# A hybrid decoder layer on one core: the merge, output projection and gate with ScalarE and VectorE in program order, and small operands prepared at other places

## The chip, the core and the metric

The kernel runs on one core of a Trainium2 chip. The core has a matrix engine (TensorE, "PE" in the profile), whose weight loads are listed apart as PEld, a vector engine (VectorE, "DVE"), a scalar engine for pointwise functions and copies (ScalarE, "ACT"), GpSimd ("POOL") and SyncE ("SP"). In this kernel GpSimd issues most weight transfers and SyncE the other transfers. The metric is the device time of one execution in microseconds (us). Before the change three runs took 463.31 to 463.59 us, with a median of 463.48 us.

## What is computed

One layer (DEPTH is 1) of a decoder on 512 tokens of width 1024. Cut to its steps:

```python
xn = rmsnorm(h, norm_gain)
aq, ak, av, ag, bq, bf, bi, bg, gate_a, gate_b = split(xn @ w_in)
ya = moba_attention(rmsnorm(aq), rmsnorm(ak), av, rel_bias)     # 8 heads x 64
ya = (ya * silu(ag)) @ w_up_a
yb = hgrn2_chunkwise(silu(bq), kb, bi, log_f)                   # 4 heads x 128
yb = (rmsnorm(yb) * silu(bg)) @ w_up_b
merged = sigmoid(gate_a) * ya + sigmoid(gate_b) * yb
h = h + merged @ w_out
ple = (p @ w_ple) * sigmoid(h @ w_ple_gate)
h = h + ple
```

All tensors are float32. Each float32 product is made of three products of rounded halves, so every operand of a matmul is first split into a high and a low part.

## The kernel before

**Splits.** `split(hi, lo, src)` (L192 to L194) is one ScalarE copy that rounds `src` to the high part (L193) and one VectorE subtraction that leaves the low part (L194). The names in the profile follow it: a raw weight `wf` becomes `wh` and `wl`; the merged rows become `mh` and `ml`; the new `h` (`hf`) becomes `hh` and `hl`; the transposed embedding `pf` becomes `ph` and `pl`; the gate's small weights `w_ple`, kept in `pb`, become `pwh` and `pwl`; the two branches' outputs become `yah`, `yal`, `ybh`, `ybl`. `mm3` (L247 to L254) multiplies: for each slice k of 128 rows it issues three matmuls of 128x512 (high by high, low by high, high by low weight), and it then ticks a planner's clock by 3 x 0.227.

**Weights.** All 80 weight tiles have a fixed sequence. `weight(ap)` returns tile i, but first loads raw tiles up to i + 2 and splits them. There are two raw buffers and three buffers each of `wh` and `wl`, so the load of tile i + 2 waits for the split of tile i, and the copy of tile i + 2 waits for the last product with tile i - 1. In the stretch at issue tiles 48 to 55 belong to the up-projections of the recurrent branch (`ub0` to `ub7`), 56 to 63 to those of attention (`ua0` to `ua7`; 128x512 each), 64 to 71 to the output projection (`h0` to `h7`; 128x1024) and 72 to 79 to the gate (`g0` to `g7`; 128x1024).

**The last stages.** `up(0, n, ya, ...)` makes `ua` number n in 12 matmuls. VectorE multiplies it by the sigmoid of gate a (L914) and adds the other branch (L915), and the result `sga` is split into `mh` and `ml` number n. Then each `h` number n needs all eight `mh` and `ml` (24 matmuls); VectorE adds the residual `xres` (L927), and the sum is split into `hh` and `hl`. Last, each `g` number n needs all eight `hh` and `hl` (24 matmuls), and beside it `pe` number n (6 matmuls) multiplies p with the small weights; ScalarE takes the sigmoid of `g`, VectorE multiplies and adds, and SyncE stores.

**The recurrence.** For each of four heads the planner runs a generator beside the projections. `hgrn_intra` builds score blocks in the PSUM banks `lpb` and `lpa`. `hgrn_out` then transposes a key block (`hktp`), copies it out by ScalarE (`hkt`, L598), multiplies it (`hds`, L603), forms the states on VectorE (L607, L610), and makes the output `hop` (L616, L618). ScalarE squares `hop` (L622); a normalisation follows that goes between VectorE and ScalarE (`npart`, `nquad`, `nms`, `nt`, `ny`, `nwide`, lines 272 to 293), and VectorE reads `hop` for the last time in L624. The banks of the tag "g" are two, so `lpa` of the next head takes the bank that L624 gives back. A `yield` in these generators is a number of microseconds of the planner's clock until the generator goes on; it sets between which matmuls its own matmuls stand.

**Attention.** `scores` (L709) makes logits `s`; the softmax runs over VectorE (L726, L729), ScalarE (L728, L730) and a VectorE transpose (L733); SyncE moves the result by 16 transfers per step within `pb` (L744); the product with the values is `o` (L757).

**What sets the order.** PE's instructions stand in the order in which the program traces them, with the planner's clock deciding where the generators' pieces go. ScalarE, VectorE, GpSimd and SyncE are ordered by a scheduler that simulates a timeline and takes what is ready by priority; `tc.high_priority(offset=AHEAD)` raises the priority of the merge. On the chip each engine works through its list in that order.

Of the kernel before, what the change touches and what calls it, by code (L numbers as in the profile page):

```python
# [20 lines left out]
KD = D // 128  # L21
# [36 lines left out]
def hybrid_layer_kernel(  # L58
# [530 lines left out]
    def hgrn_out(h, vb):  # L589
# [6 lines left out]
        cost(0.33)  # L596
        kts = unit("KT", f"hkt{h}")
        A.activation(kts[:, :nk], kt[:, :nk], AF.Copy)  # L598
        yield 4.0
        hv = slice(h * 128, h * 128 + 128)  # L600
        dsp = bank("g", f"hds{h}")
        for c in range(3):
# [288 lines left out]
    for kind, i in ORDER:  # L891
        if kind == "bf":
            head(i)
        elif kind == "bg":
            sbgs.append(silu_block(12 + i, f"bg{i}"))
        elif kind == "ag":
            sags.append(silu_block(8 + i, f"ag{i}"))
        elif kind == "ub":
            drain(f"yb{GH - 1}")
            ps = up(1, i, yb, f"ub{i}")  # L900
            V.tensor_tensor(sg["gb", i], ps, sg["gb", i], op=OP.mult)
        else:
            ps = proj_tr({"ga": 16, "gb": 24}[kind] + i, f"{kind}{i}")
            sg[kind, i] = unit("A" if kind == "ga" and i < 4 else "H", f"s{kind}{i}")
            sigmoid(sg[kind, i], ps)
    mh, ml = [], []
    for n in range(KD):
        ga, gb = sg["ga", n], sg["gb", n]
        drain(f"ya{HPAIRS - 1}")
        ps = up(0, n, ya, f"ua{n}")  # L910
        h_ = unit("YB", f"mh{n}", R)
        l_ = unit("A", f"ml{n}", R)
        with tc.high_priority(offset=AHEAD):
            V.tensor_tensor(ga, ps, ga, op=OP.mult)  # L914
            V.tensor_tensor(ga, ga, gb, op=OP.add)  # L915
            split(h_, l_, ga)
        mh.append(h_)
        ml.append(l_)
    hh, hl, hf = [], [], []
    for n in range(KD):  # L920
        ws = weight(w_o[n])
# [9 lines left out]
        hh.append(h_)  # L931
        hl.append(l_)
        hf.append(t)
    ph, pl = [], []
    for k in range(2):
        t = unit("A", f"pf{k}")
        for i in range(2 - k):
            w = 256 * (1 + k)
            nc.sync.dma_start(t[:, w * i:w * i + w], pT[:, k, w * i:w * i + w])
        h_ = unit("A", f"ph{k}", R)  # L940
        l_ = unit("A", f"pl{k}", R)
        split(h_, l_, t)
        ph.append(h_)
        pl.append(l_)
    for n in range(KD):
        if n % 2 == 0:
            pw = pb[:, n // 2].rearrange("p (a b c) -> p a b c", a=2, b=2)
            nc.sync.dma_start(pw, w_p[n // 2])
            pwh = unit("SG", f"pwh{n}", R, (128, 2, 2, 128))
            pwl = unit("T", f"pwl{n}", R, (128, 2, 2, 128))  # L950
            split(pwh, pwl, pw)
        ws = weight(w_g[n])
        pe = bank("a", f"pe{n}")
        parts = 1 if n < KD - 1 else 2
        w = 512 // parts
        for i in range(parts):
            s_ = slice(i * w, i * w + w)

            def ple():
                mm3(pe[:, s_], pwh[:, n % 2], pwl[:, n % 2], [a[:, s_] for a in ph], [a[:, s_] for a in pl], 2)  # L960

            last = i == 1
            if not last:
                ple()
            ps = bank("mm", f"g{n}_{i}")
            mm3(ps[:, :w], ws[0], ws[1], [a[:, s_] for a in hh], [a[:, s_] for a in hl], KD)
            if last:
                ple()
            t = unit("Q", f"sg{n}_{i}")
            A.activation(t[:, :w], ps[:, :w], AF.Sigmoid)  # L970
            V.tensor_tensor(t[:, :w], t[:, :w], pe[:, s_], op=OP.mult)
            V.tensor_tensor(t[:, :w], t[:, :w], hf[n][:, s_], op=OP.add)
            nc.sync.dma_start(out[n][:, s_], t[:, :w])
# [66 lines left out]
```

## Time and profile before

| what | value |
|---|---|
| runs | 463.31, 463.48, 463.59 us |
| the profiled execution, its own time | 463.43 us |
| its span in the profile | 461.7 us |
| TensorE busy | 454.5 us, 98% of the span |
| PE weight loads | 375.9 us, 81% |
| VectorE busy | 297.7 us, 64% |
| ScalarE busy | 276.3 us, 60% |
| `ua` (first to last start) | 335.5 to 357.1 us |
| `h` | 357.3 to 402.9 us |
| `pe` and `g` | 402.9 to 457.7 us |

The span runs from the first to the last recorded instruction; 1.73 us of the execution lie outside it. In the timeline views a row gives the start, the duration, the engine, the line, the operation, the output and inputs, their shapes and a count; in brackets stands how long the engine was idle before and what ended that. Matmuls of 128x512 overlap: each is listed with 0.39 us, while one starts every 0.227 us.

### The profile page before, as it was taken

The page shows a single profiled execution, that of the slowest core. Times are in us where ns is not written, and L with a number is a line of the kernel's source. Part 1 is how long each engine was busy: PE and PEld are TensorE (multiplying, and loading weights), DVE is VectorE, ACT ScalarE, POOL GpSimd, SP SyncE. Part 2 cuts the span into 40 slices and gives each one's busy share as a digit, 9 for nine tenths or more (in the row PEclk, how much of TensorE's full clock was granted, in tenths as well). Part 3 has the DMA queues.
Part 4 walks back from the last instruction along what each step waited for, and adds up shares of the span by engine and source line. Part 5 has one row for each costly group of instructions (what it writes and reads, how often), then busy time and mean ns, then how long its engine had stood idle before and what let it go on. Part 6 is the DMA issues. An engine that isn't in the chain of part 4 may idle for free.

```text
span 461.7 us, 8102 instructions
## 1 busy us (share of the span) xinstructions
PE 454.5 (98%) x3106; PEld 375.9 (81%) x3106; DVE 297.7 (64%) x604; ACT 276.3 (60%) x532; POOL 38.5 (8%) x77
## 2 busy tenths in 40 slices
PE   9999999999999999999999999999999899999996
PEld 8787888888888888788878888878888688888886
DVE  5668593876888594969686945454469644544222
ACT  5758574747689795979788777774334423322201
POOL 1000100000000101000101000001121100000000
PEclk9999999999999999999999999999999999999999
DMA  7822242220412525162415351335334554222211
GB/s 241 296 91 100 92 136 92 91 92 22 146 65 91 161 99 177 23 182 96 134 56 156 93 179 52 115 119 148 121 91 147 185 165 144 91 103 83 89 45 45
DMA packets 23590, 53.72 MB, mean 116 GB/s; under 512 B 4352, under 2 KB 9728, under 8 KB 23552
## 3 DMA queue, kind: packets, MB, share of 16 engines
q0 software_dynamic: 9056, 32.51, 21.3%
q1 hardware_dynamic: 14352, 20.70, 14.4%
q8 instruction: 24, 0.39, 0.4%
q14 instruction: 14, 0.11, 0.1%
q10 hardware_dynamic: 144, 0.01, 0.0%
HBM read 45.86 MB, written 2.10 MB: 104 GB/s over the span
## 4 chain that ended last, share of the span: by engine, by line
PE 86%; DMA 5%; ACT 5%; issue 2%; DVE 1%; SPq 1%; POOL 0%; POOLq 0%; DVEq 0%; ACTq 0%
PE ga L252 10%; PE g L252 9%; PE gb L252 9%; PE h L252 8%; PE bq L252 5%; PE ak L382 5%; PE ub L252 5%; PE aq L382 5%; PE bf L252 5%; PE bg L252 4%; PE av L382 4%; PE bi L382 4%; PE ag L252 3%; PE pe L252 2%; DMA wf<-in_w_tok_dram 2%
## 5 line engine op out<-in xcount | busy, mean ns | idle before, releaser
L193 ACT ACTIVATE wh<-wf 128x1024 fp32r<-128x1024 f32 (+1 forms) x78 | 75.6, 970 | 102.1 <-PE g L252 20.9
L194 DVE TENSOR_TENSOR wl<-wf,wh 128x1024 fp32r<-128x1024 f32 (+1 forms) x78 | 86.6, 1112 | 64.1 <-ACT wh L193 63.6
L226 POOL DMA_DIRECT2D wf<-in_w_tr_dram x30 | 15.9, 530 | 175.0 <-DVE wl L194 156.6
L252 PE MATMUL g<-hh,wh 128*128 128x512 f32 (+1 forms) x72 | 26.3, 365 | 0.0
L252 PE MATMUL g<-hl,wh 128*128 128x512 f32 (+1 forms) x72 | 26.3, 365 | 0.0
L252 PE MATMUL g<-hh,wl 128*128 128x512 f32 (+1 forms) x72 | 26.3, 365 | 0.0
L252 PE MATMUL h<-ml,wh 128*128 128x512 f32 x64 | 25.0, 391 | 0.8 <-DVE ml L194 0.8
L252 PE MATMUL ga<-xh,wh 128*128 128x512 f32 x64 | 25.7, 401 | 0.0
L252 PE MATMUL h<-mh,wh 128*128 128x512 f32 x64 | 25.0, 391 | 0.5 <-ACT mh L193 0.5
L252 PE MATMUL gb<-xh,wh 128*128 128x512 f32 x64 | 25.0, 391 | 0.0
L252 PE MATMUL ga<-xh,wl 128*128 128x512 f32 x64 | 25.0, 390 | 0.0
L252 PE MATMUL ga<-xl,wh 128*128 128x512 f32 x64 | 25.0, 390 | 0.0
L252 PE MATMUL gb<-xh,wl 128*128 128x512 f32 x64 | 24.9, 389 | 0.0
L252 PE MATMUL gb<-xl,wh 128*128 128x512 f32 x64 | 24.9, 389 | 0.0
L252 PE MATMUL h<-mh,wl 128*128 128x512 f32 x64 | 24.9, 389 | 0.0
L728 ACT ACTIVATE pb<-pb,ps 128x128 f32<-128x128 f32 (+3 forms) x32 | 17.6, 552 | 9.7 <-DVE ps L726 9.6
L726 DVE CUSTOM_DVE_ANT_0 pb<-s,bias 128x128 f32<-128x128 f32 (+3 forms) x28 | 12.8, 496 | 10.2 <-PE s L709 10.0
L927 DVE TENSOR_TENSOR hf<-h,xres 128x512 f32<-128x512 f32 x8 | 5.5, 692 | 18.0 <-PE h L252 18.0
L497 ACT ACTIVATE hx<-hx 128x512 f32<-128x512 f32 x24 | 14.8, 622 | 1.9 <-DVE hx L496 1.8
L730 ACT ACTIVATE pb<-pb,ps 128x128 f32<-128x128 f32 (+3 forms) x32 | 15.8, 550 | 0.0
L252 PEld LDWEIGHTS g<-hl,wh 128*128 128x128 f32 x72 | 13.6, 189 | 2.2
L252 PEld LDWEIGHTS g<-hh,wl 128*128 128x128 f32 x72 | 13.6, 189 | 2.2
(343 smaller groups left out, 1250.3 us busy)
## 6 DMA issues: line engine op xcount, KB each, us to landing
wf<-in_w_tr_dram POOLq DMA_DIRECT2D x30, 512.0 KB, 4.0
wf<-in_w_tok_dram POOLq DMA_DIRECT2D x8, 512.0 KB, 3.6
wf<-in_w_up_dram POOLq DMA_DIRECT2D x16, 256.0 KB, 3.0
wf<-in_w_o_dram POOLq DMA_DIRECT2D x8, 512.0 KB, 4.1
wf<-in_w_g_dram POOLq DMA_DIRECT2D x8, 512.0 KB, 3.5
wf<-in_w_tok_dram SPq DMA_DIRECT2D x6, 512.0 KB, 3.8
pb<-pb SPq DMA_DIRECT2D x64, 48.0 KB, 2.6
bias<-in_ed_dram SPq DMA_DIRECT2D x8, 256.0 KB, 5.0
```

The source lines that it names most:

```text
L193: A.activation(hi, src, AF.Copy)
L194: V.tensor_tensor(lo, src, hi.bitcast(F32), op=OP.subtract)
L226: (G if len(wraw) >= FAR else nc.sync).dma_start(raw, ap)
L252: PE.matmul(ps, a[:, k, :], b[k], start=(n == 0), stop=(n == tot - 1))
L382: PE.matmul(banks[t], a[:, s_], b[:, kk, :], start=(k == 0 and i == 0), stop=(k == KD - 1 and i == 2))
L497: A.activation(x, x, AF.Exp)
L726: in_order(V.tensor_tensor_reduce(p_, s_[:, so:so + nk], T[j][:, nk - 1::-1], -1.0, 3e38, OP.add, OP.min, st[:, 0:1]))
L728: A.activation(p_, p_, AF.Exp, bias=st[:, 0:1], scale=-1.0, accum_out=st[:, 1:2])
L730: A.activation(p_, p_, AF.Copy, scale=st[:, 2:3])
L927: V.tensor_tensor(t, ps, xres, op=OP.add)
```

## The change

It has three parts.

1. In `hgrn_out` the wait between the copy of `hkt` and the product `hds` is 5.0 instead of 4.0 on the planner's clock.
2. From attention's up-projections on, ScalarE and VectorE too stand in the order of the program (`manual_schedule`); the raised priority of the merge is gone with that.
3. The transfers and splits of p (`positions`) are traced behind `h3` and `h4` instead of behind `h7`; the split of the first small weight (`ple_weight`) is traced behind `h5`, and the others one pair of gate tiles ahead, behind the products of `g0`, `g2` and `g4`.

```diff
--- before.py
+++ after.py
@@ -596,7 +596,7 @@
         cost(0.33)
         kts = unit("KT", f"hkt{h}")
         A.activation(kts[:, :nk], kt[:, :nk], AF.Copy)
-        yield 4.0
+        yield 5.0
         hv = slice(h * 128, h * 128 + 128)
         dsp = bank("g", f"hds{h}")
         for c in range(3):
@@ -903,6 +903,8 @@
             ps = proj_tr({"ga": 16, "gb": 24}[kind] + i, f"{kind}{i}")
             sg[kind, i] = unit("A" if kind == "ga" and i < 4 else "H", f"s{kind}{i}")
             sigmoid(sg[kind, i], ps)
+    ctx.enter_context(tc.manual_schedule(engines={mybir.EngineType.Activation, mybir.EngineType.DVE}))
+
     mh, ml = [], []
     for n in range(KD):
         ga, gb = sg["ga", n], sg["gb", n]
@@ -910,12 +912,34 @@
         ps = up(0, n, ya, f"ua{n}")
         h_ = unit("YB", f"mh{n}", R)
         l_ = unit("A", f"ml{n}", R)
-        with tc.high_priority(offset=AHEAD):
-            V.tensor_tensor(ga, ps, ga, op=OP.mult)
-            V.tensor_tensor(ga, ga, gb, op=OP.add)
-            split(h_, l_, ga)
+        V.tensor_tensor(ga, ps, ga, op=OP.mult)
+        V.tensor_tensor(ga, ga, gb, op=OP.add)
+        split(h_, l_, ga)
         mh.append(h_)
         ml.append(l_)
+    ph, pl = [], []
+
+    def positions(k):
+        t = unit("A", f"pf{k}")
+        for i in range(2 - k):
+            w = 256 * (1 + k)
+            nc.sync.dma_start(t[:, w * i:w * i + w], pT[:, k, w * i:w * i + w])
+        h_ = unit("A", f"ph{k}", R)
+        l_ = unit("A", f"pl{k}", R)
+        split(h_, l_, t)
+        ph.append(h_)
+        pl.append(l_)
+
+    pws = {}
+
+    def ple_weight(n):
+        pw = pb[:, n].rearrange("p (a b c) -> p a b c", a=2, b=2)
+        nc.sync.dma_start(pw, w_p[n])
+        pwh = unit("SG", f"pwh{n}", R, (128, 2, 2, 128))
+        pwl = unit("T", f"pwl{n}", R, (128, 2, 2, 128))
+        split(pwh, pwl, pw)
+        pws[n] = pwh, pwl
+
     hh, hl, hf = [], [], []
     for n in range(KD):
         ws = weight(w_o[n])
@@ -931,25 +955,13 @@
         hh.append(h_)
         hl.append(l_)
         hf.append(t)
-    ph, pl = [], []
-    for k in range(2):
-        t = unit("A", f"pf{k}")
-        for i in range(2 - k):
-            w = 256 * (1 + k)
-            nc.sync.dma_start(t[:, w * i:w * i + w], pT[:, k, w * i:w * i + w])
-        h_ = unit("A", f"ph{k}", R)
-        l_ = unit("A", f"pl{k}", R)
-        split(h_, l_, t)
-        ph.append(h_)
-        pl.append(l_)
+        if n in (3, 4):
+            positions(n - 3)
+        if n == 5:
+            ple_weight(0)
     for n in range(KD):
-        if n % 2 == 0:
-            pw = pb[:, n // 2].rearrange("p (a b c) -> p a b c", a=2, b=2)
-            nc.sync.dma_start(pw, w_p[n // 2])
-            pwh = unit("SG", f"pwh{n}", R, (128, 2, 2, 128))
-            pwl = unit("T", f"pwl{n}", R, (128, 2, 2, 128))
-            split(pwh, pwl, pw)
         ws = weight(w_g[n])
+        pwh, pwl = pws[n // 2]
         pe = bank("a", f"pe{n}")
         parts = 1 if n < KD - 1 else 2
         w = 512 // parts
@@ -966,6 +978,8 @@
             mm3(ps[:, :w], ws[0], ws[1], [a[:, s_] for a in hh], [a[:, s_] for a in hl], KD)
             if last:
                 ple()
+            if i == 0 and n % 2 == 0 and n < KD - 2:
+                ple_weight(n // 2 + 1)
             t = unit("Q", f"sg{n}_{i}")
             A.activation(t[:, :w], ps[:, :w], AF.Sigmoid)
             V.tensor_tensor(t[:, :w], t[:, :w], pe[:, s_], op=OP.mult)
```

What this does to the engines' lists is shown at three places. The number behind an underscore counts tiles and may differ between the two lists; the number ahead of it is that of the projection, head or weight.

**VectorE at the end of attention's up-projections.** `sga` is the gated sum, `ml` its low part, `wl64` to `wl66` are the low parts of the first weights of the output projection. Before:

```order
L194 TENSOR_TENSOR wl64_3894<-wf64_3891,wh64_3893 128x1024
L914 TENSOR_TENSOR sga6_3516<-ua6_3897,sga6_3516 128x512
L194 TENSOR_TENSOR ml5_3886<-sga5_3445,mh5_3885 128x512
L194 TENSOR_TENSOR wl65_3919<-wf65_3916,wh65_3918 128x1024
L915 TENSOR_TENSOR sga6_3516<-sga6_3516,sgb6_3046 128x512
L914 TENSOR_TENSOR sga7_3551<-ua7_3922,sga7_3551 128x512
L915 TENSOR_TENSOR sga7_3551<-sga7_3551,sgb7_3093 128x512
L194 TENSOR_TENSOR ml6_3911<-sga6_3516,mh6_3910 128x512
L194 TENSOR_TENSOR wl66_3944<-wf66_3941,wh66_3943 128x1024
L194 TENSOR_TENSOR ml7_3936<-sga7_3551,mh7_3935 128x512
```

After:

```order
L194 TENSOR_TENSOR wl64_3896<-wf64_3893,wh64_3895 128x1024
L915 TENSOR_TENSOR sga6_3516<-ua6_3899,sga6_3516 128x512
L916 TENSOR_TENSOR sga6_3516<-sga6_3516,sgb6_3046 128x512
L194 TENSOR_TENSOR ml6_3913<-sga6_3516,mh6_3912 128x512
L194 TENSOR_TENSOR wl65_3921<-wf65_3918,wh65_3920 128x1024
L915 TENSOR_TENSOR sga7_3551<-ua7_3924,sga7_3551 128x512
L916 TENSOR_TENSOR sga7_3551<-sga7_3551,sgb7_3093 128x512
L194 TENSOR_TENSOR ml7_3938<-sga7_3551,mh7_3937 128x512
L194 TENSOR_TENSOR wl66_3946<-wf66_3943,wh66_3945 128x1024
```

Before, a weight's subtraction or the next multiplication stands between most steps of one merge, and `wl66` stands ahead of `ml7`. Now the multiplication, the addition and the low part of one number follow one another, and the weight's subtraction comes behind them. ScalarE's list there is `mh5`, `wh64`, `mh6`, `wh65`, `mh7`, `wh66` now, and was `wh64`, `mh5`, `wh65`, `mh6`, `wh66`, `mh7`.

**TensorE at the second head (number 1) of the recurrence.** `hds1` is the product that reads `hkt1`; `ag2` and `gb3` are projections. Before:

```order
L252 MATMUL ag2_2084<-xl6_461,wh30_1846 128x512
L252 MATMUL ag2_2084<-xh6_460,wl30_1847 128x512
L603 MATMUL hds1_2125<-biv0_391,hkt1_2092 128x128
L603 MATMUL hds1_2125<-biv1_393,hkt1_2092 128x128
L603 MATMUL hds1_2125<-biv2_395,hkt1_2092 128x128
L252 MATMUL ag2_2084<-xh7_485,wh30_1846 128x512
L252 MATMUL ag2_2084<-xl7_486,wh30_1846 128x512
L252 MATMUL ag2_2084<-xh7_485,wl30_1847 128x512
L252 MATMUL gb3_2147<-xh0_412,wh31_1887 128x512
```

After:

```order
L252 MATMUL ag2_2084<-xl6_461,wh30_1846 128x512
L252 MATMUL ag2_2084<-xh6_460,wl30_1847 128x512
L252 MATMUL ag2_2084<-xh7_485,wh30_1846 128x512
L252 MATMUL ag2_2084<-xl7_486,wh30_1846 128x512
L252 MATMUL ag2_2084<-xh7_485,wl30_1847 128x512
L252 MATMUL gb3_2139<-xh0_412,wh31_1887 128x512
L252 MATMUL gb3_2139<-xl0_413,wh31_1887 128x512
L252 MATMUL gb3_2139<-xh0_412,wl31_1888 128x512
L603 MATMUL hds1_2143<-biv0_391,hkt1_2092 128x128
L603 MATMUL hds1_2143<-biv1_393,hkt1_2092 128x128
L603 MATMUL hds1_2143<-biv2_395,hkt1_2092 128x128
L252 MATMUL gb3_2139<-xh1_420,wh31_1887 128x512
```

The three rows of `hds1` stand six matmuls later; `hop1` moves by six too, and so do `hds` and `hop` of heads 2 and 3. The rows of the scores, of `lpb`, `lpa` and `o` keep their places.

**ScalarE and VectorE in the normalisation of head 2.** `ho2` is the square of `hop2`; `nquad`, `nt`, `ny`, `nwide` are the steps of its normalisation; `wh41` is a weight and `sga0` the sigmoid of a gate. ScalarE before:

```order
L622 ACTIVATE ho2_2800<-hop2_2792 128x512
L277 ACTIVATE nquad_2806<-npart_2804 32x16 x4
L193 ACTIVATE wh41_2860<-wf41_2858 128x1024
L263 ACTIVATE nt_2814<-nms_2811,epsc_82 32x16
L257 ACTIVATE sga0_2854<-ga0_2777 128x512
L264 ACTIVATE ny_2813<-nt_2814 32x16
L258 ACTIVATE sga0_2854<-sga0_2854,onec_84 128x512
L259 ACTIVATE sga0_2854<-sga0_2854 128x512
L292 ACTIVATE nwide_2821<-ny_2813 32x16 x4
```

ScalarE after:

```order
L622 ACTIVATE ho2_2812<-hop2_2804 128x512
L193 ACTIVATE wh41_2860<-wf41_2858 128x1024
L257 ACTIVATE sga0_2854<-ga0_2777 128x512
L277 ACTIVATE nquad_2818<-npart_2816 32x16 x4
L258 ACTIVATE sga0_2854<-sga0_2854,onec_84 128x512
L263 ACTIVATE nt_2826<-nms_2823,epsc_82 32x16
L259 ACTIVATE sga0_2854<-sga0_2854 128x512
L264 ACTIVATE ny_2825<-nt_2826 32x16
L292 ACTIVATE nwide_2833<-ny_2825 32x16 x4
```

VectorE before, from the last step of the normalisation:

```order
L293 STREAM_TRANSPOSE hy2_2801<-nwide_2821 128x512
L624 SCALAR_TENSOR_TENSOR ho2_2800<-hop2_2792,sm_66,hy2_2801 128x512
L630 TENSOR_TENSOR bg2s_2073<-bg2s_2073,ho2_2800 128x512
L726 ISA pb_68,ps230_2894<-s210_2886,bias20_2540 128x512
L726 ISA ps230_2894 128x1
L726 ISA pb_68,ps231_2900<-s211_2887,bias21_2542 128x512
```

VectorE after:

```order
L293 STREAM_TRANSPOSE hy2_2813<-nwide_2833 128x512
L726 ISA pb_68,ps230_2894<-s210_2886,bias20_2540 128x512
L726 ISA ps230_2894 128x1
L624 SCALAR_TENSOR_TENSOR ho2_2812<-hop2_2804,sm_66,hy2_2813 128x512
L726 ISA pb_68,ps231_2900<-s211_2887,bias21_2542 128x512
L726 ISA ps231_2900 128x1
```

On ScalarE the copy of weight 41 and the exponential of gate 0 (L257) now stand ahead of `nquad`. On VectorE the first half of the softmax step (L726 of `ps230`) now stands ahead of L624, the last reader of `hop2`. At head 1 ScalarE's list changes in the same way, with weight 34 and gate b3.

## The prediction

> **What bounds the kernel now.** I read the page first, then the waits of TensorE, then its timeline at each wait.
>
> ```profile
> span 461.7 us, 8102 instructions
> PE 454.5 (98%) x3106; PEld 375.9 (81%) x3106; DVE 297.7 (64%) x604; ACT 276.3 (60%) x532; POOL 38.5 (8%) x77
> L252 PE MATMUL h<-ml,wh 128*128 128x512 f32 x64 | 25.0, 391 | 0.8 <-DVE ml L194 0.8
> ```
>
> TensorE is busy for 98%: its matmuls set the end, their number does not change, and only its waits can be won or lost. In the timeline of its starts (one matmul of 128x512 every 0.227 us) I find two places where the change moves a wait: the end of `h0` and the product `hds`. First `h0`, with what ScalarE and VectorE did there:
>
> ```profile
> 361.84 0.39 PE L252 MATMUL h<-mh,wl 128*128 128x512 f32 x1
> 362.70 0.49 PE L252 MATMUL h<-mh,wh 128*128 128x512 f32 x1 [0.48 <-ACT mh L193]
> 364.05 0.50 PE L252 MATMUL h<-ml,wh 128*128 128x512 f32 x1 [0.85 <-DVE ml L194]
> ...
> 361.07 1.06 ACT L193 ACTIVATE wh<-wf 128x1024 fp32r<-128x1024 f32 x1 [2.12 <-DMA wf<-in_w_o_dram]
> 362.04 0.61 ACT L193 ACTIVATE mh<-sga 128x512 fp32r<-128x512 f32 x1
> ...
> 362.17 1.22 DVE L194 TENSOR_TENSOR wl<-wf,wh 128x1024 fp32r<-128x1024 f32 x1 [1.95 <-ACT wh L193]
> 363.31 0.68 DVE L194 TENSOR_TENSOR ml<-sga,mh 128x512 fp32r<-128x512 f32 x1
> ```
>
> Without waits the matmul with `ml7` would start two steps behind 361.84, at 362.29; it starts at 364.05, so 1.76 us are lost. The reader is to see why: `mh7` and `ml7` stand behind weight 66, whose transfer lands only at 361.07.
>
> **The merge in program order.** The inversion goes: `mh7` and `ml7` now stand ahead of `wh66` and `wl66`. But each number now is a chain in which VectorE waits for ScalarE, and the next multiplication stands behind it all. The pieces of that chain:
>
> ```profile
> 338.26 0.39 PE L252 MATMUL ua<-yah,wh 128*128 128x512 f32 x1
> ...
> 338.46 0.69 DVE L914 TENSOR_TENSOR sga<-ua,sga 128x512 f32<-128x512 f32 x1 [1.43 <-PE ua L252]
> 339.07 0.68 DVE L194 TENSOR_TENSOR wl<-wf,wh 128x512 fp32r<-128x512 f32 x1
> 339.67 0.68 DVE L915 TENSOR_TENSOR sga<-sga,sgb 128x512 f32<-128x512 f32 x1
> ...
> 358.21 0.68 DVE L914 TENSOR_TENSOR sga<-ua,sga 128x512 f32<-128x512 f32 x1
> 358.93 0.69 DVE L915 TENSOR_TENSOR sga<-sga,sgb 128x512 f32<-128x512 f32 x1
> ...
> 328.73 0.63 ACT L193 ACTIVATE yah<-ag3s 128x512 fp32r<-128x512 f32 x1 [2.39 <-DVE ag3s L761]
> 340.39 0.63 ACT L193 ACTIVATE mh<-sga 128x512 fp32r<-128x512 f32 x1 [1.52 <-DVE sga L915]
> ...
> 329.40 0.69 DVE L194 TENSOR_TENSOR yal<-ag3s,yah 128x512 fp32r<-128x512 f32 x1 [0.70 <-ACT yah L193]
> ```
>
> From start to start: multiplication to dependent addition 0.72 (358.21 to 358.93), addition to `mh` 0.72 (339.67 to 340.39), high to low part 0.67 (328.73 to 329.40), `ml` to the weight's subtraction 0.60 and that to the next multiplication 0.60 (as 339.07 to 339.67). The weight's copy stands behind `mh` on ScalarE, 0.6 later, and its subtraction is ready just then. The sum is 3.31 us per number. TensorE makes one `ua` in 12 x 0.227 = 2.72 (`ua0` is done when `ua1` starts at 338.26). So VectorE falls 0.59 behind per number. The sums of work alone (four operations at 0.60 on VectorE) would fit into 2.72; the 0.9 us that VectorE waits within the chain does not.
>
> From `ml5` on the weight is a 128x1024 one: its copy starts 2.0 after the multiplication and lasts 1.06, so the subtraction starts at 3.10, and it holds VectorE for 1.14 (362.17 to 363.31): 4.24 per number. With the first multiplication at 338.46, number 5 starts at 338.46 + 5 x 3.31 = 355.01, number 6 at 359.25 and number 7 at 363.49; `ml7` starts 2.11 later and is done at 366.28, TensorE goes on at 366.34. That is 366.34 - 364.05 = **2.29 us later than now**, though the inversion is gone. TensorE loses that time in pieces: `h0` is due at 357.30 and gets `wh64` at 358.1 and `wl64` at 359.3 (they stand behind `ml5`), then `mh7` at 365.6. The transfers of the weights should not enter:
>
> ```profile
> wf<-in_w_o_dram POOLq DMA_DIRECT2D x8, 512.0 KB, 4.1
> ...
> 355.65 5.32 DMA wf<-in_w_o_dram
> ```
>
> Tile 64 is issued when `wl62` frees its buffer, at about 352.1, so it lands near 356.2, and its turn on ScalarE comes at 357.0; tile 65 is issued at 355.4 and has until 361.2. Ends: if each handover (eight numbers, about one tenth each) is shorter than read, the loss falls to 1.5; if weight 64 takes the 5.32 us of tile 66 and ScalarE's slack there is used up, it rises to 2.9. I take 2.3, since every piece has its own row.
>
> **`hds` six matmuls later.** Two waits of TensorE end:
>
> ```profile
> 192.42 0.39 PE L252 MATMUL ag<-xh,wl 128*128 128x512 f32 x1
> 193.36 0.82 PE L603 MATMUL hds<-biv,hkt 128*128 128x128 f32 x5 [0.55 <-ACT hkt L598]
> ...
> 241.29 0.39 PE L252 MATMUL ag<-xh,wl 128*128 128x512 f32 x1
> 241.77 0.94 PE L603 MATMUL hds<-biv,hkt 128*128 128x128 f32 x6
> ```
>
> Less the pitch of 0.227, head 1 loses 0.71 and head 2 0.25. Six matmuls are 1.36 us, so both go: at most 0.96. Behind the first stands another wait:
>
> ```profile
> 231.75 1.53 PE L757 MATMUL o<-pb,avv 128*64 128x128 f32 x24
> 233.58 1.09 PE L757 MATMUL o<-pb,avv 128*64 128x128 f32 x16 [0.30 <-DMA pb<-pb]
> ...
> 220.93 30.69 SPq L744 DMA_DIRECT2D pb<-pb  x32
> ...
> 207.40 0.75 DVE L624 SCALAR_TENSOR_TENSOR ho<-hop,sm,hy 128x512 f32<-128x512 f32 x1
> 219.57 1.30 DVE L733 STREAM_TRANSPOSE pb<-pb 128x512 f32<-128x512 f32 x2
> ```
>
> The second half of `o1` waits for the transfers of its softmax, which start when VectorE's transposes end (220.9), and between L624 and them VectorE is never idle (its busy time is 13.43 of 13.47 us, the fourth figure of the row):
>
> ```profile
> 207.40:220.87 13.47, 13.47 (x184) 11.12 (x184) 13.43 (x33) 12.73 (x27) 0.53 (x1) 1.00 0.27 93
> ```
>
> So a later L624 makes the transfers later by as much, and TensorE arriving 0.71 earlier only waits longer. L624 itself comes later: ScalarE's `nquad` now stands behind weight 34 and a gate's exponential; by the same reckoning as for head 2 below it moves from 207.40 to about 207.7. So at `o1` TensorE is **0.3 later** (ends: 0.4 earlier, 0.9 later), whatever it won at head 1. Head 2 then gives back **0.25**.
>
> **The bank of `hop2`.** `lpa` of head 3 takes the bank that L624 releases:
>
> ```profile
> 247.31 0.39 PE L618 MATMUL hop<-ha,st 128*128 128x128 f32 x2
> 257.76 0.45 PE L518 MATMUL lpa<-hx 128*32 128x16 f32 x32
> ...
> 249.83 0.95 ACT L277 ACTIVATE nquad<-npart 32x16 f32<-32x16 f32 x4 [1.50 <-DVE npart L274]
> 250.96 1.06 ACT L193 ACTIVATE wh<-wf 128x1024 fp32r<-128x1024 f32 x1 [0.18 <-PE ga L252]
> 252.12 0.57 ACT L257 ACTIVATE sga<-ga 128x512 f32<-128x512 f32 x1
> ...
> 255.68 0.75 DVE L624 SCALAR_TENSOR_TENSOR ho<-hop,sm,hy 128x512 f32<-128x512 f32 x1
> ```
>
> Now L624 ends at 256.43 and `lpa` starts at 257.76: 1.3 us of room. In the change `hop2` ends 1.36 later, and `nquad` stands behind weight 41, which waits for TensorE's gate product until 250.96, and behind the exponential: 250.96 + 1.06 + 0.57 less 0.1 each for overlap, 252.4 instead of 249.83, is 2.6 later. Between `nquad` and L624 the copy, VectorE's subtraction for weight 41 and the exponential stand no longer. They took 249.83 to 255.68, 5.85 us, of which at most 1.1 (the subtraction) lay on the chain, since the copy and the exponential ran beside it. Two steps of the gate's sigmoid still stand between `nt` and `ny`, about 0.5 more than now, and an L726 (0.6) stands ahead of L624. 2.6 - 1.1 + 0.5 + 0.6 = 2.6 makes 256.43 to 259.0; placing each step behind its two predecessors instead gives 258.8, since ScalarE's steps overlap. `lpa` is due at 257.8 (257.76 and the 0.05 from above): **1.0 us lost**. Ends: 0 (the room of 1.3 just holds) and 1.5. What is late next is the second half of head pair 2's softmax step and so `o2`, which shows no wait now.
>
> **Steps at no cost.** p's splits and the small weights (0.6 us on each engine for each) are covered by `h` and `pe` with `g`, 5.4 and 6.8 us per number against some 3.5 us of VectorE work; uncovered, all six would cost 3.6. On SyncE p's transfers stand ahead of `xres3` and `xres6`, needed a stage (5.4 us) or more later. The small weights' copies leave ScalarE's list at `ub`, where it idles.
>
> **Sum.** 0.3 - 0.25 + 1.0 + 2.3 = 3.3 us. Against the profiled execution: span 461.7 + 3.3 = 465.0, and with the 1.73 outside it 463.43 + 3.3 = **466.7 us**. The median of the runs, 463.48, stands 0.05 above that execution.
>
> **Rivals.**
>
> *Only the end slips* (465.5): the recurrence keeps its room, and -0.25 + 2.3 remain. For it: the 1.0 us at `lpa` is the small difference of two long sums, and 1 us too much in one of them ends it; it decides from an end of L624 at 257.8. Against it: `nquad` cannot run ahead of a copy that waits for TensorE.
>
> *The merge keeps pace*: VectorE's four operations run at 0.60 each, ScalarE's copies beside them, and a number takes no more than 2.72. Then `ml7` is done about 2.9 us after `ua7` ends at 357.5, before it is due at 362.29; the 1.76 and 0.25 are won, 463.43 - 2.0 = 461.4. It decides from 7 periods that sum to 20.9, that is 2.99 us per number: below, `h0` ends earlier than now. Against it: the rows of the lists leave nothing for VectorE to do while it waits for `mh`.
>
> *The moves cancel* (463.6): a period of about 3.0 us, so that `h0` ends as now, no loss at `lpa`, and the two gains of `hds` lost at `o1`. The rows speak against the first of these as they do above.
>
> *The clock falls* (468.5): gaps at `h0` sum to 4.0 us within 9. If TensorE then runs at half its clock for as long as the gaps lasted, nine matmuls take 0.227 more each, 2.0, less what is hidden. The trace speaks against it: the 1.8 us lost there now are followed by a window of full clock.
>
> ```profile
> 360.00:380.00 20.00, 18.67 (x81) 14.90 (x80) 10.71 (x14) 7.36 (x10) 2.12 (x4) 1.00 0.44 144
> ```
>
> [...]
>
> **How the numbers follow.** Forecast 0.56, only the end slips 0.20, clock 0.05, a mix of these at 464.5 to 468 0.01; keeps pace 0.08, cancel 0.10 (one part in ten of it below the bound). A measurement of this kernel can tell 0.2%, 0.93 us: 462.55 to 464.41 counts as no change. So slower 0.82, same 0.09, faster 0.09. The range takes the ends of the terms (-0.4 to 0.9, -0.25, 0 to 1.5, 1.5 to 2.9: 0.85 to 5.05) and leaves out the outermost fifth: 464.6 to 468.0.
>
> **What would show it.** In the changed profile: VectorE's multiplications in the merge 3.3 us apart and 4.2 at the end; TensorE's rows of `h0` waiting for `wh`, `wl`, then `mh` and `ml`, the last at about 367.4 (366.3 plus the 1.05 lost before); `hds` without a wait; `lpa` of head 3 with about 1 us of idle time released by VectorE; `o1` still waiting for its transfers, over a us. The forecast is wrong if the multiplications follow TensorE's 2.72, or if `lpa` starts without a wait.

## The result and the profile after

The changed kernel takes 466.94 us (median of 6 runs, 466.30 to 469.44); the kernel before took 463.39 us in the same comparison (6 runs, 462.69 to 463.90). The ratio is 1.0086, with a 95% interval of 1.0061 to 1.0111: slower, by 3.55 us between the medians. The forecast was 466.7 us.

The top of the profile page of the changed kernel, and of its groups the product with `mh` in `h`, which lost 0.8 us to waits before:

```profile
span 466.1 us, 8103 instructions
PE 456.4 (98%) x3106; PEld 377.0 (81%) x3106; DVE 298.9 (64%) x604; ACT 275.4 (59%) x532; POOL 38.4 (8%) x77
L252 PE MATMUL h<-mh,wh 128*128 128x512 f32 x64 | 25.9, 404 | 2.0 <-ACT mh L193 1.6
```

TensorE is still busy for 98%, and its busy time itself has grown by 1.9 us with the same 3106 instructions; that will matter below. TensorE's waits in the changed kernel (total, times, longest):

```profile
PE h L252 <- ACT mh L193: 1.6, 1, 1.6
PE o L757 <- DMA pb<-pb: 1.4, 1, 1.4
PE lpa L518 <- DVE ho L624: 0.9, 1, 0.9
...
PE h L252 <- DVE wl L194: 0.5, 1, 0.5
PE h L252 <- ACT wh L193: 0.4, 1, 0.4
PE h L252 <- DVE ml L194: 0.2, 1, 0.2
```

The wait of `hds` is gone, `o` waits over a us, `lpa` waits for L624, and `h` waits for `wh`, `wl`, `mh` and `ml`. To put numbers on them, the two timelines must be laid over one another. TensorE's rows before, and the same instructions after (the first is `bg` ahead of head 1's `hds`, the next two stand at `h0`, the last is `pe0`, behind all of `h`):

```profile
186.69 0.50 PE L252 MATMUL bg<-xh,wh 128*128 128x512 f32 x1
...
357.30 0.39 PE L252 MATMUL h<-mh,wh 128*128 128x512 f32 x1
...
402.74 0.39 PE L252 MATMUL pe<-ph,pwh 128*128 128x512 f32 x1
```

```profile
186.32 0.50 PE L252 MATMUL bg<-xh,wh 128*128 128x512 f32 x1
...
193.62 0.83 PE L603 MATMUL hds<-biv,hkt 128*128 128x128 f32 x6
...
233.59 1.09 PE L757 MATMUL o<-pb,avv 128*64 128x128 f32 x16 [1.39 <-DMA pb<-pb]
258.43 0.45 PE L518 MATMUL lpa<-hx 128*32 128x16 f32 x32 [0.85 <-DVE ho L624]
...
358.81 0.50 PE L252 MATMUL h<-mh,wh 128*128 128x512 f32 x1 [0.37 <-ACT wh L193]
360.07 0.50 PE L252 MATMUL h<-mh,wl 128*128 128x512 f32 x1 [0.53 <-DVE wl L194]
366.26 0.49 PE L252 MATMUL h<-mh,wh 128*128 128x512 f32 x1 [1.60 <-ACT mh L193]
366.98 0.50 PE L252 MATMUL h<-ml,wh 128*128 128x512 f32 x1 [0.23 <-DVE ml L194]
...
407.24 0.39 PE L252 MATMUL pe<-ph,pwh 128*128 128x512 f32 x1
```

Ahead of everything the change touches, this execution runs 0.37 us early (186.32 against 186.69; the kernel before had lost that at its start). So 0.37 is added to each shift. At `o1` the second half starts 233.59 + 0.37 - 233.58 = 0.38 later than before, although `hds` won 0.7. The first product with `ml7` starts 366.98 + 0.37 - 364.05 = 3.30 later, and `pe0` 407.24 + 0.37 - 402.74 = 4.87 later. The 3.30 up to the end of the holes is the forecast's 3.3. The 1.57 between them is not in the sum, and no wait stands there: TensorE runs without a stop, but slowly. The windows around it (span of the window, then each engine's busy time with its count, and behind POOL the granted clock, DMA share and GB/s):

```profile
360.00:365.00 5.00, 4.59 (x19) 3.49 (x19) 3.97 (x7) 1.58 (x2) 1.02 (x2) 1.00 0.33 107
365.00:367.00 2.00, 0.51 (x2) 0.20 (x2) 1.23 (x2) 1.43 (x2) 0.04 (x1) 1.00 0.61 174
367.00:371.00 4.00, 4.00 (x11) 3.17 (x12) 2.87 (x4) 1.73 (x3) 0.53 (x1) 0.57 0.29 93
371.00:375.00 4.00, 4.00 (x19) 3.33 (x18) 1.08 (x2) 0.00 (x0) 0.53 (x1) 1.00 0.83 270
```

Right behind the hole at 366 the granted clock is 0.57 in the mean of four us, and 1.00 again from 371 on; it is 0.50 from 367.41 to 370.82. Seven starts from 367.66 to 370.65 are 0.427 us apart, instead of 0.227. Over this whole run the clock is 0.996. Of the six runs two have 0.996 (467.92, which is the profiled one, and 469.44 us); the other four, at 0.999 to 1.0, took 466.30 to 467.14, with a median of 466.56, 3.17 us above the kernel before. So the forecast's terms make up the four runs, and the clock comes on top in the two others; 469.44 is 2.9 us above that median, more than the 1.6 of one such stretch, and what else it holds is not known.

VectorE's multiplications of the merge, the first two and the last three:

```profile
339.14 0.69 DVE L915 TENSOR_TENSOR sga<-ua,sga 128x512 f32<-128x512 f32 x1 [1.43 <-PE ua L252]
...
342.46 0.68 DVE L915 TENSOR_TENSOR sga<-ua,sga 128x512 f32<-128x512 f32 x1
...
355.74 0.68 DVE L915 TENSOR_TENSOR sga<-ua,sga 128x512 f32<-128x512 f32 x1
...
359.93 0.68 DVE L915 TENSOR_TENSOR sga<-ua,sga 128x512 f32<-128x512 f32 x1
...
364.13 0.68 DVE L915 TENSOR_TENSOR sga<-ua,sga 128x512 f32<-128x512 f32 x1
...
366.24 0.69 DVE L194 TENSOR_TENSOR ml<-sga,mh 128x512 fp32r<-128x512 f32 x1 [0.69 <-ACT mh L193]
```

They stand 3.32 us apart, and 4.19 and 4.20 at the end (forecast 3.31 and 4.24), while TensorE makes a `ua` in 2.72: the chain of VectorE and ScalarE sets the pace. That it is the chain and not the amount of work is argued here and tested below.

### The profile page after: what moved, and what is told of

It reads as the page before. It is cut to its first block, busy times and chain, and to the rows that moved or that the text cites. A ratio compares the mean times of both kernels' runs of the same rounds, so it can differ in the third digit from the quotient of the medians.

```text
span 466.1 us, 8103 instructions
## 1 busy us (share of the span) xinstructions
PE 456.4 (98%) x3106; PEld 377.0 (81%) x3106; DVE 298.9 (64%) x604; ACT 275.4 (59%) x532; POOL 38.4 (8%) x77
## 4 chain that ended last, share of the span: by engine, by line
PE 86%; DVE 5%; ACT 5%; SPq 2%; issue 1%; DMA 1%; DVEq 0%
PE g L252 9%; PE h L252 9%; PE ga L252 8%; PE gb L252 7%; PE ak L382 5%; PE ub L252 5%; PE aq L382 5%; PE av L382 5%; PE bf L252 5%; PE ag L252 5%; PE bi L382 4%; PE bg L252 4%; PE bq L252 4%; PE pe L252 2%; PE o L757 2%; SPq L744 2%
## 5 line engine op out<-in xcount | busy, mean ns | idle before, releaser
L984 ACT ACTIVATE sg<-g 128x512 f32<-128x512 f32 (+1 forms) x9 | 5.0, 550 | 39.6 <-PE g L252 39.6
L985 DVE TENSOR_TENSOR sg<-sg,pe 128x512 f32<-128x512 f32 (+1 forms) x9 | 5.7, 628 | 33.0 <-ACT sg L984 30.7
L728 ACT ACTIVATE pb<-pb,ps 128x128 f32<-128x128 f32 (+3 forms) x32 | 17.7, 553 | 12.8 <-DVE ps L726 12.8
L193 ACT ACTIVATE hh<-hf 128x512 fp32r<-128x512 f32 x8 | 5.1, 632 | 28.4 <-DVE hf L951 28.4
L726 DVE CUSTOM_DVE_ANT_0 pb<-s,bias 128x128 f32<-128x128 f32 (+3 forms) x28 | 12.9, 494 | 9.1 <-PE s L709 9.0
L193 ACT ACTIVATE mh<-sga 128x512 fp32r<-128x512 f32 x8 | 5.1, 632 | 19.8 <-DVE sga L916 19.8
L252 PEld LDWEIGHTS h<-mh,wh 128*128 128x128 f32 x64 | 12.4, 193 | 5.3 <-ACT mh L193 2.0
```

The lines of the kernel that those rows point to most:

```text
L193: A.activation(hi, src, AF.Copy)
L252: PE.matmul(ps, a[:, k, :], b[k], start=(n == 0), stop=(n == tot - 1))
L726: in_order(V.tensor_tensor_reduce(p_, s_[:, so:so + nk], T[j][:, nk - 1::-1], -1.0, 3e38, OP.add, OP.min, st[:, 0:1]))
L728: A.activation(p_, p_, AF.Exp, bias=st[:, 0:1], scale=-1.0, accum_out=st[:, 1:2])
```

## The experiments

The theory that they test: the cost is the sum of separate terms (at `o1`, at `lpa`, at `h0`), each from one part of the change. The rivals are named with each run. "Holes" are TensorE's starts in the timeline less the pitch, "restart" the 0.11 us by which the first matmul behind a hole is longer (0.50 for 0.39, as in the rows above).

**Part 1 alone.**

```diff
 (on the kernel before, in hgrn_out)
-        yield 4.0
+        yield 5.0
```

> The kernel before, with part 1 alone (hds and hop six matmuls later). Theory (the terms add): hds of heads 1 and 2 starts without a wait (0.71 and 0.25 won), the second half of o1 waits 1.0 to 1.5 us for its transfers, so the 0.71 is lost again, lpa of head 3 waits 0.8 to 1.0 us for L624, and h0 loses its 1.75 us as before: +0.7, about 464.1 us. Rival (the recurrence keeps its room without the new order at the end): no wait at lpa, 463.1 us or less. In both the clock is 1.00 behind h0.

Measured: 463.29 us against 463.71; ratio 1.0008 (0.9981 to 1.0035). One of the twelve runs took 468.93 us at a clock of 0.992; it was not profiled, so where its clock fell is not known. TensorE's waits, all of a tenth and more behind the start:

```profile
PE o L757 <- DMA pb<-pb: 1.0, 1, 1.0
PE lpa L518 <- DVE ho L624: 0.9, 1, 0.9
...
PE h L252 <- DVE ml L194: 0.2, 1, 0.2
```

The recurrence does what the theory says: `hds` does not wait, `o1` and `lpa` do, and at `ua0` TensorE is 1.02 us behind the kernel before (336.23 against 335.54, and 0.33 early at the start). But `h0`, which this edit does not touch, lost 0.31 instead of 1.75, so that the time does not show the loss. The lists of ScalarE and VectorE at the end are those of the kernel before; what differed was the transfer of weight 66. From its issue to ScalarE's copy it took 5.42 us in the profile before and 4.24 here. Both kernels were profiled once more for that.

> The run with part 1 alone once more, to see whether h0's wait is steady. Theory (it hangs on how long the transfer of weight 66 takes beside p's three transfers, 4.2 us there and 5.4 before): anything between 0.3 and 1.8 us, going with the landing of weight 66. Rival (it is the later hds that ends it): 0.3 us again.

> The kernel before once more, for the same question: theory, h0's wait lies between 0.3 and 1.8 us and goes with the landing of weight 66; rival, 1.75 us again, as the same program does the same.

Each was timed once, beside its profile: 462.69 us for part 1 alone, 462.32 us for the kernel before. Issue and copy of weight 66 in the latter:

```profile
355.04 0.53 POOL L226 DMA_DIRECT2D wf<-in_w_o_dram  x1 [4.27 <-DMA wf<-in_w_o_dram]
```

```profile
359.94 1.06 ACT L193 ACTIVATE wh<-wf 128x1024 fp32r<-128x1024 f32 x1 [1.31 <-DMA wf<-in_w_o_dram]
```

With the run below there are five profiled executions with the old order at the end. In them weight 66 took 4.24, 4.37, 4.90, 5.42 and 5.43 us from issue to copy, and `h0` lost 0.31, 0.49, 1.32, 1.75 and 1.90: the wait goes with the transfer, as the theory had it. The two short ones are both those of part 1 alone, so the rival (the later `hds` ends it) is not excluded; in those two weight 66 was issued 0.16 and 0.20 us behind p's transfers on SyncE, in the others 0.42 to 0.56 behind. Why this matters to the transfer was not tried. What follows for the forecast: the 1.76 us that it took from one profile as what `h0` loses now is not steady.

**`hop` at its place before.**

```diff
 (on part 1 alone)
-        yield 3.0
+        yield 2.0
         op_ = bank("g", f"hop{h}")
```

> The kernel before, with hds six matmuls later, but hop of heads 1 to 3 at its place before (the wait between them is one microsecond of the planner's clock shorter). ScalarE's nquad of head 2 stands ahead of weight 41 again. Theory (lpa waits because hop and with it nquad come later): hds without a wait, lpa of head 3 without a wait, o1 still waits over 1 us for its transfers, so that of 0.96 only 0.25 is kept: 463.2 us. Rival (hop then waits for the states, since VectorE has six matmuls less for them): a wait of hop of 0.3 us or more, 463.5 us or more.

Measured: 462.52 us, ratio 0.9973 (0.9959 to 0.9987). In the profile `lpa` does not wait: with the same later `hds`, the 0.95 us vanish with `hop`'s place. That shows the mechanism of this term: `hop` and with it `nquad` come later, and the bank comes free later. `hop` waits for nothing over 0.15 us. `o1` lost 0.49, not over 1 as expected: head 1's L624 was 0.36 us earlier than before (206.60 with 0.44 of lead, against 207.40), and the transfers with it. The idle time there, 0.38, is hardly more than the 0.30 of the kernel before, so most of what `hds` won is kept: at `ua0` TensorE is 0.63 us ahead of the kernel before (334.47 and the lead, against 335.54).

**Parts 2 and 3 without part 1.**

```diff
 (on the changed kernel, in hgrn_out)
-        yield 5.0
+        yield 4.0
```

> The changed kernel, with hds back at its place before: parts 2 and 3 alone. Theory (the terms add): the waits of hds are back, lpa of head 3 does not wait, VectorE's multiplications of the merge stand 3.32 us apart and 4.2 at the end, ml7's first matmul comes 2.2 to 2.3 us later than before: 465.6 us, and up to 1.6 more in runs in which TensorE's clock falls behind h0. Rival (the three parts need each other): the end slips by less than 1.5 us since the recurrence is earlier, 464.5 us or less. On the clock: if the holes of h0 (3.5 us in 9) make it fall, then here too in a part of the runs; if the fall came from elsewhere, the clock stays at 1.00 here.

Measured: 466.25 us, ratio 1.0065 (1.0041 to 1.0089). The waits of the end are those of the whole change, within 0.02 us (1.76 for `mh`, 0.69 for `wl`, 0.54 for `wh`, 0.50 for `ml`), and `lpa` does not wait. The clock falls here too, without any change in the recurrence:

```profile
365.00:370.00 5.00, 4.78 (x13) 3.57 (x14) 3.79 (x5) 2.40 (x3) 0.53 (x1) 0.66 0.43 139
```

Three of the six runs have a clock of 0.996 (466.66, 467.52 and 467.68 us); the others took 465.30, 465.73 and 465.85. The middle one, 465.73, is what the theory said without the clock (465.6). So nearly all of the slowdown belongs to parts 2 and 3, and the rival (an end that slips by less than 1.5) falls. The run without the moves, below, has the same holes at `h0` with part 2 alone (0.51, 0.69, 1.71 and 0.50).

**The weight's split within the merge.** This is the test of the chain, since it adds and removes no operation:

```diff
 (on parts 2 and 3 without part 1, in the loop of the merge)
         V.tensor_tensor(ga, ga, gb, op=OP.add)
+        if n < KD - 1:
+            w_split(wpos[0] + LD)
         split(h_, l_, ga)
```

> As the run with parts 2 and 3 alone, but in the merge of each number but the last the split of the next weight is traced between the addition and the split of the sum: ScalarE copies the weight beside VectorE's multiplication and addition, and VectorE subtracts it while it would wait for mh. Theory (the chain sets the pace: 0.72 + 0.72 + 0.60 + 0.67, about 2.71 us per number, under TensorE's 2.72): multiplications follow ua, 2.72 apart, h0 waits for nothing or under 0.3 us, 1.75 us less than before: 461.7 us, and the clock stays at 1.00. Rival (not the chain but the weights' transfers or ScalarE's order set the pace at the end): h0 still waits for wh64, wl64 or wh65, at least 1.2 us, 463 us or more.

Measured: 461.40 us, ratio 0.9957 (0.9942 to 0.9972), faster than the kernel before (463.71 in this comparison) and 4.85 us below the run without the edit, 4.33 below the middle one of that run's executions with a full clock. One period of the merge, and its end:

```profile
341.26 0.69 DVE L915 TENSOR_TENSOR sga<-ua,sga 128x512 f32<-128x512 f32 x1
341.98 0.69 DVE L916 TENSOR_TENSOR sga<-sga,sgb 128x512 f32<-128x512 f32 x1
342.59 0.68 DVE L194 TENSOR_TENSOR wl<-wf,wh 128x512 fp32r<-128x512 f32 x1
...
343.37 0.69 DVE L194 TENSOR_TENSOR ml<-sga,mh 128x512 fp32r<-128x512 f32 x1
343.98 0.68 DVE L915 TENSOR_TENSOR sga<-ua,sga 128x512 f32<-128x512 f32 x1
...
360.85 0.69 DVE L194 TENSOR_TENSOR ml<-sga,mh 128x512 fp32r<-128x512 f32 x1 [0.70 <-ACT mh L193]
```

The subtraction of the weight fills the time in which VectorE waited for `mh`; the period is 2.72, TensorE's own, and `ml7` is done at 361.5, before TensorE reads it at 362.4. `h0` waits for nothing, and all eight runs have a clock of 0.998 or above. The rival (transfers set the pace) falls. With this the reason for the forecast's largest term is shown: not the amount of work on VectorE, which is the same in both, but the place of the wait within the chain.

**The changed kernel with that line.** All three parts, and the two lines above.

> The changed kernel (all three parts) with one line mended: the next weight's split stands between the addition and the split of the sum. Theory (terms add): the end wins 1.75, the recurrence loses 1.05 as in the change (lpa waits 0.95, o1 1.1 longer, hds 0.96 won): 462.5 us and a full clock behind h0. Rival (a later start of the merge gives other lists or other collisions): h0 waits again over 0.5 us, 463.2 us or more.

Measured: 462.52 us, ratio 0.9968 (0.9950 to 0.9985). Its waits are those of the recurrence alone:

```profile
PE o L757 <- DMA pb<-pb: 0.9, 1, 0.9
PE lpa L518 <- DVE ho L624: 0.9, 1, 0.9
```

The terms of the recurrence and of the end add, as the theory says; the change misses its gain by one place in a list.

**That line, with later `hds` and `hop` in place.**

> The run with the weight's split between addition and split, with hds six matmuls later and hop at its place besides. Theory (the two gains add): no wait at h0, none at hds and lpa, 0.4 to 0.6 us less than without the later hds: 460.9 us. Rival (the transfers of o1 take the gain back): 461.4 us, with a wait of 1 us or more at o1.

Measured: 461.33 us, ratio 0.9939 (0.9919 to 0.9959). In the profile the waits of `hds`, `o1` and `lpa` are all gone, and `hop` waits 0.32 once: by its holes it should be 0.7 us faster than the run without the later `hds`, while the medians differ by 0.07. Over six and eight runs that scatter by a us and more this is not told apart, so what the later `hds` is worth on top of that line stays open. On the old order at the end, with `hop` in place, it is worth something: the run above is at 0.9973 of the kernel before, with an interval below 1.

**The order without the moves.** Part 2 alone: p's splits behind `h7`, each small weight ahead of its gate tiles.

```diff
 (on parts 2 and 3 without part 1)
-        if n in (3, 4):
-            positions(n - 3)
-        if n == 5:
-            ple_weight(0)
+    for k in range(2):
+        positions(k)
     for n in range(KD):
+        if n % 2 == 0:
+            ple_weight(n // 2)
         ws = weight(w_g[n])
...
-            if i == 0 and n % 2 == 0 and n < KD - 2:
-                ple_weight(n // 2 + 1)
```

> As the run with parts 2 and 3 alone, but without part 3: p's splits stay behind h7, and each small weight's split ahead of its pair of gate tiles, in the order of the program. Theory (with the program's order the moves carry the gate): pe0 waits for hh7, ph0, ph1 and pwh0 on ScalarE, about 3.4 us after h7; pe2, pe4 and pe6 wait for the sigmoid, pwh and pwl behind it, about 2.35 us each: 3.4 + 7.0 = 10.4 us more than with the moves, about 476.7 us. Rival (the moves cost and win nothing, as the free steps of the prediction would have it): 466.3 us, as with them.

Measured: 481.63 us (two runs, 479.29 and 483.98), ratio 1.0372 (1.0324 to 1.0421). TensorE's waits:

```profile
PE pe L252 <- ACT pwh L193: 6.6, 4, 3.0
PE pe L252 <- DVE pwl L194: 2.6, 4, 0.8
```

The holes at `pe0`, `pe2`, `pe4` and `pe6` sum to 10.6 us, as the theory said; the medians differ by 5 us more. In the profile the clock falls three times at the gate, to 0.50 for 3.41 or 3.42 us, which is 1.6 us each; the windows stand below. So with the program's order part 3 is what keeps the gate from losing 10 us. That it wins nothing of its own is likely, since the kernel before has no waits there, but part 3 was not tried without part 2.

**What makes the clock fall.** Three runs open a hole of a chosen size at `mh7`, where the weight's split within the merge leaves none:

```diff
 (on the run with the weight's split within the merge; K is 6, 4 and 10)
+        for _ in range(K if n == KD - 1 else 0):
+            A.activation(h_, ga, AF.Copy)
         split(h_, l_, ga)
```

> The run with the weight's split between, with six more ScalarE copies of the same rows ahead of mh7 (0.53 us each, so mh7 3.2 us later), which open one hole of about 1.9 us ahead of the matmul with mh7 and one of 0.35 behind it; no other waits in h0. It asks what makes TensorE's clock fall behind h0. Theory A (a hole of two us is enough, now and then): in about a third of the runs the clock falls, 0.996 over the run and 1.5 us more: 463.7 us, else 465.2. Theory B (it takes the waits for wh64 and wl64 ahead of it, 3.5 us in sum): no run falls, 463.7 us. [...]

> As the run with one hole, but four extra copies instead of six (0.66 us each there): holes of 1.1 us ahead of mh7's matmul and 0.5 behind it. Theory (the clock is set anew every 3.41 us, and falls for one such stretch when TensorE stood idle for about 1.9 us or more of the one before): never 1.9 us within 3.41, so no run falls; 463.1 us (461.4 + 1.6 and the restarts), all clocks at 0.998 or above. Rival (any stop of a us can make it fall): some runs at 0.996 and 1.6 us more.

> As the run with one hole, but ten extra copies: a hole of 5.05 us ahead of mh7's matmul. Theory (3.41 us stretches): at least one stretch lies with 1.9 us or more of idle time wherever the stretches begin, so every run falls; 464.4 + 2.65 = 467.1 us without the clock and up to 1.6 more, less what of the slow stretch lies within the hole itself: 467.1 to 468.7, clocks at 0.996 or between that and 1.0. Rival (chance): a part of the runs only, as with the hole of 2.4.

| extra copies | holes at `mh7` and `ml7` | time, ratio to before | runs with a clock of 0.996 or less |
|---|---|---|---|
| 4 | 1.17 and 0.50 | 463.20, 1.0002 (0.9987 to 1.0017) | 0 of 10 |
| 6 | 2.40 and 0.49 | 466.49, 1.0052 (1.0036 to 1.0067) | 7 of 10 |
| 10 | 4.98 and 0.50 | 469.70, 1.0148 (1.0107 to 1.0189) | 4 of 4, all at 0.993 |

The six copies took 0.66 us each instead of 0.53, so that hole was larger than meant. One hole of 2.40 us with 0.49 behind it, and no waits ahead of it, is enough: theory B falls. The clock falls in 7 of those 10 runs, and in none of the 10 with 1.17 and 0.50. With 4.98 it falls in all four, and by more than expected: 469.7 is 2.6 us above the 467.1 without it, and in the profile the matmuls stand 0.43 us apart from 368.6 to about 373.5, longer than one stretch of 3.41, where the theory had counted on one. The granted clock is 0.50 there from 366.66 to 373.48, 6.82 us, which is two stretches of 3.41. The first of them held only the last 0.61 us of the long hole and the 0.50 behind it, and yet the clock stayed down for the second; why is not shown.

When it fell can be read from the run without the moves, which has four falls in one execution. Windows over them, and one window in between (the granted clock stands third from the end):

```profile
367.64:371.06 3.42, 3.42 (x9) 2.64 (x8) 2.47 (x4) 1.58 (x2) 0.53 (x1) 0.50 0.31 86
412.02:415.43 3.41, 3.41 (x9) 2.63 (x9) 0.21 (x1) 0.25 (x1) 0.53 (x1) 0.50 0.43 145
429.08:432.50 3.42, 3.42 (x9) 2.64 (x9) 0.85 (x1) 0.00 (x0) 0.53 (x1) 0.50 0.47 151
446.15:449.57 3.42, 2.95 (x13) 2.46 (x14) 1.55 (x2) 0.00 (x0) 0.00 (x0) 1.00 0.20 77
463.22:466.63 3.41, 3.41 (x10) 2.64 (x9) 0.00 (x0) 0.00 (x0) 0.00 (x0) 0.50 0.14 54
```

The clock is at half (0.50) in the whole of four of them, and full (1.00) in the one between. The half stretches end at 371.06, 415.43, 432.50 and 466.63, which lie 44.4, 17.1 and 34.1 us apart: 13, 5 and 10 times 3.41. In the changed kernel the clock is at half from 367.41 to 370.82 and, behind the last matmul, again from 466.40, which is 95.57 us or 28 times 3.413 after 370.82. An interval is here such a stretch of 3.41 us, counted on or back from the end of a half one. A half stretch loses 3.41 x (1 - 0.227 / 0.427) = 1.6 us, with the two distances of starts from the changed kernel's rows; that kernel lost 1.57. Counted back, the intervals ahead of the four falls held holes of 2.2, 1.88, 2.33 and 2.34 us. The pair of holes that did not make it fall has the same shape as two that did:

```profile
443.49 0.39 PE L252 MATMUL g<-hh,wl 128*128 128x512 f32 x1
445.08 0.50 PE L252 MATMUL pe<-ph,pwh 128*128 128x512 f32 x1 [1.21 <-ACT pwh L193]
445.42 0.39 PE L252 MATMUL pe<-pl,pwh 128*128 128x512 f32 x1
446.62 0.50 PE L252 MATMUL pe<-ph,pwl 128*128 128x512 f32 x1 [0.80 <-DVE pwl L194]
```

There the border of an interval, at 446.15, cuts the second hole, and the fuller interval held 1.87. So the least that was followed by a fall in this execution is 1.88 us of holes, and this count does not part it from the 1.87 that was not. Counted from each matmul's recorded end to the next start, over all whole intervals of the fourteen profiles up to the last matmul, the two are apart: intervals with 1.71 us of idle time or more were followed by a fall (1.83 in the changed kernel), and in these profiles a full clock never fell behind one with 1.54 or less (1.33 at most in the kernel before).

So in these profiles the falls go with the idle time within one interval of 3.41 us. That the border lies elsewhere from run to run, so that the same program falls in one and not in another, is an inference from them. The profiled execution with six copies, which kept its clock, shows it:

```profile
362.77 0.39 PE L252 MATMUL h<-mh,wl 128*128 128x512 f32 x1
365.40 0.51 PE L252 MATMUL h<-mh,wh 128*128 128x512 f32 x1 [2.24 <-ACT mh L193]
366.12 0.50 PE L252 MATMUL h<-ml,wh 128*128 128x512 f32 x1 [0.22 <-DVE ml L194]
```

Counted back in whole intervals from 463.39, where the clock of this execution falls behind its last matmul, a border lies at 364.40 and cuts the hole of 2.40 into 1.40 and 1.00. If the border can lie anywhere, and a fall takes an amount of idle time between the 1.54 and the 1.71 counted above, the rows give falls in 72 to 81% of the executions with six copies, in 39 to 63% with the end of the changed kernel, and in none with four copies (an estimate from these profiles). The runs have 7 of 10, 5 of 12 and 0 of 10.

## Why the prediction was right

By its own steps:

- **The merge chain, 2.29.** Right, in size and in mechanism. The periods came out at 3.32 and 4.20 for 3.31 and 4.24, and `ml7`'s first product at 366.98, which with the 0.37 of lead is 367.35, for the forecast's 367.4. TensorE is 1.04 behind at `ua0` (336.21 and the lead, against 335.54) and 3.30 at `ml7`: 2.26 us lie between. The split within the merge shows that it is the chain: the same work in another place runs at 2.72.
- **What this is measured against** was not steady, which the forecast did not see: `h0` lost 1.75 us in the one profile that it read, and 0.3 to 1.9 in the five profiled executions of the old order. The two at the kernel before itself gave 1.75 and 1.32.
- **The bank of `hop2`, 1.0.** Right: 0.95 in this kernel, in part 1 alone (0.95 both times) and in the changed kernel with the weight's split within the merge (0.95), and nothing once `hop` is put back. L624 ended at 258.29, with the lead 258.66, for 258.8.
- **`o1`, 0.3 later.** The number came true in this execution (0.38) but the step behind it did not: head 1's L624 did not move by 0.3 but by 0.07 (207.10 and the lead of 0.37, against 207.40). In the runs with part 1 alone and in the changed kernel with the weight's split within the merge `o1` came 0.05, 0.12 and 0.18 earlier. What holds is that the 0.71 us of `hds` are lost again at the transfers while `hop` stands later too, and that their end moves by some tenths from run to run; with `hop` back at its place most of them are kept.
- **Head 2 gives back 0.25.** Right: no wait of `hds` is left.
- **Steps at no cost.** Right as to the moves; the forecast did not say that they are needed: without them the program's order loses 10.6 us at the gate, while the 3.6 us named for the case that they lost their cover counted only their work, not the waits that follow one another there.
- **The clock falls** (chance 0.05) is the step that failed. The half clock behind the gaps of `h0`, which the author put there as an "if", is in the trace: 0.50 for one interval of 3.41 us, which cost 1.57, not for as long as the gaps lasted, for which the forecast had put 2.0. A clock of 0.996 was found in 2 of 6 runs of the change and in 3 of 6 with parts 2 and 3. The forecast let itself be talked out of it by a row of full clock behind the 1.8 us lost before; beyond that row the 0.05 is the author's estimate. But the 0.63 and 1.12 lost before, both within one interval, make 1.75, less than the 1.88 that was the least ahead of a fall in the run without the moves (3 of the 25 runs of the kernel before in one comparison have 0.996; where their clock fell is not known), and 1.67 made it fall in none of ten runs, while the changed kernel's 1.76 and 0.49, with 1.2 us ahead of them, make 2.25. With 2.40 and 0.49 us, with no holes ahead of them, it fell in 7 of 10.

The median stayed near the forecast because four of the six runs kept their clock. That is luck: at the estimated 39 to 63%, four of the six could as well have fallen, and the median would have come near 468 (466.56 and 1.6).

## What to carry to other kernels

An engine that keeps pace by its sum of work need not keep pace in program order: add up the chain from one stage's first instruction to the next stage's, with the waits for the other engine in it, and look for an operation that can stand in such a wait. Here moving one subtraction and its copy into it turned 466.25 us into 461.40, where the kernel before took 463.71. A hole on TensorE can cost more than its length: here one of 2.40 us, with 0.49 behind it, was followed by a lower clock in 7 of 10 runs, and a half stretch cost 1.6 us. So behind a hole of some two us, look at the granted clock of the next four us, and in several runs.

## What was not expected of the hardware

- The granted clock was at half for 3.41 or 3.42 us at a time in the changed kernel and in the run without the moves, and for 6.82 behind a hole of 4.98. The four stretches of the run without the moves end 13, 5 and 10 times 3.41 us apart. Each cost some 1.6 us (worked out from 3.41 us with the matmuls 0.427 instead of 0.227 apart; 1.57 was lost in the changed kernel), and the intervals ahead of them held holes of 1.88 to 2.34 us. Of three pairs of holes of one shape in that execution, two were followed by a fall and one was not.
- A transfer of 512 KB with the same place in its list took 4.24 to 5.43 us from issue to use in five profiled executions, and the waits of `h0` beside it differed by up to 1.6 us; one profile of a wait that ends in a DMA is a sample, not a constant.
